# All sixteen gate blocks in seven-product steps, with the attention's filler dealt by eighths

## The chip, the cores and the metric

The kernel runs on one core of a Trainium2 chip. TensorE multiplies matrices (PE in the profile; PEld is its weight load), VectorE (DVE), ScalarE (ACT) and GpSimd (POOL) do the other arithmetic, and SyncE (SP) mostly issues transfers (DMA). Each engine runs its own queue in order and waits for the others by semaphores. The metric is the device time of one execution in microseconds, the median of several runs; lower is better.

## The reference

One layer of a streaming encoder on x of 512 tokens by 1024 features, in float32:

```python
h = rms_norm(x, norm_mix_g)
cb, cc, cin, q, k, v, f_logit, g_logit = split(h @ w_in)      # 3 x 512 | 3 x 512 | 8 | 2 x 1024
y_conv = (cb * causal_dwconv(cc * cin)) @ w_out_conv
o = forgetting_attention(q, k, v, log_sigmoid(f_logit + b_f))   # 8 heads of 64, blocks of 128 queries
y_attn = o @ w_out_attn
g_conv, g_attn = split(sigmoid(g_logit + b_gate))
x = x + (g_conv * y_conv + g_attn * y_attn) @ w_o
h = rms_norm(x, norm_ffn_g)
a, b = split(causal_dwconv(h @ w_up))                          # 2 x 2816
x = x + (silu(a) * b) @ w_down
return rms_norm(x, norm_f_g)
```

## The kernel before

Everything is held transposed, features on the 128 partitions and the 512 tokens along the free axis, so x is eight blocks of 128 x 512. Every product is made of three: weights and activations are split into a high part (a copy rounded to fp32r) and a low part (the difference), and `mm3` (L301) multiplies high by high, low by high and high by low, 256 columns at a time. A weight chunk of 128 x 1024 is loaded by SP into a ring (`load`, L169; four buffers for the tag "raw"), split by ScalarE (L275) and VectorE (L279) in `split`, and used in the order of one list, `stream`.

A *seven-product step* (`seven`, L824) replaces a 2 x 2 arrangement of blocks, which takes eight block products, by seven. Its weights come as P chunks (blocks used as they are) and F chunks (sums of blocks). The sums are made in DRAM ahead of time: `make_forms` (L190) queues for each group of steps a chain of six transfers, alternately a copy issued by SP (`put`, L208) and an adding transfer issued by GpSimd (`add`, L211), and `slot` (L218) releases those that are due by a running count. On the activations' side the step needs the differences of x's quarter blocks, made in `xt` by `x_scale` and `x_sums` during the attention and split into high and low parts `xth` and `xtl` by `x_split` (L899).

The stages in order:

1. *v and forget logits* (L452): x and the weights arrive in eight blocks; TensorE runs some warm-up matmuls on constants first (`NWARM`, L113). The first block's weights come in two transfers, one by ScalarE's queue and one by SP's, and are cast in two pieces.
2. *queries and keys 0 and 1*: four projections of 48 matmuls each.
3. *attention* (L795): 37 slots written out by hand. Slot i issues the scores of unit i (a head and a block of 128 queries), one piece of filler, the transposes of unit i - 3 and, where two query blocks of two heads are complete, the attend of unit i - 5. The filler is a list of halves of projections (24 matmuls): the convolutions' twelve, queries and keys 2 and 3, and the two gate blocks of j = 0 (in20 and in28). GpSimd multiplies the exponentials by the reciprocal of their sum (L625) before the transposes.
4. *gates and mix* (L959): for each of eight j a pair of gate blocks, then `yc` and `ya` (48 matmuls), the sigmoids and the weighted sum. `GJ = 2`: j = 0 takes the gates made in the attention, j = 1 makes them by two plain projections (`p_ga`, `p_gb`), and j = 2 to 7 by a seven-product pair. Temporaries of the gates lie in `xm`, which later holds x again.
5. *w_o*, the second norm (`rstd_col`, `rstd_bc`, L338 to L367: the reciprocal roots are spread over the partitions by matmuls with a broadcast column against the identity), the channel mixer in two phases, the last eight products, and the final norm, among whose steps `warm_on` (L1436) puts matmuls that nobody reads.

TensorE's instructions, the weights' loads and the splits of the first stage are kept in the order of the program (`keep`); the other instructions are placed by the framework. `later`, `run_later` and `flush` hold back evacuation work and release it behind splits.

Of the kernel before, what the change touches and what calls it, by code (L numbers as in the profile page):

```python
# [8 lines left out]
F32 = mybir.dt.float32  # L9
# [4 lines left out]
P = 128  # L14
D = 1024
S = 512
# [11 lines left out]
NWARM = 8  # L28
# [3 lines left out]
PADL, PADR = 16, 120  # L32

# [21 lines left out]
GJ = 2  # L55
# [11 lines left out]
GROUPS = {"gate": (2, 4, 1), "up0": (2, 4, 1), "up1": (2, 4, 1), 0: (2, (0, 3, 14, 18, 22, 26), 1), 1: (2, 3, 1)}  # L67
# [3 lines left out]
def block_kernel(ctx, tc, xT, vecs, wv, win, wmix, wo, wup, wst, wdp, outT):  # L71
# [36 lines left out]

    tbl = cp.tile([4 * H, 1], F32, tag="tbl", name="tbl")
# [14 lines left out]
    late = conv_i[0] + qk_i[2] + conv_i[1] + qk_i[3] + conv_i[2] + conv_i[3] + [20, 28]  # L124
# [8 lines left out]
    for j in range(KB):  # L133
        if j >= GJ:
            stream += step_chunks(n) + step_chunks(n + 1)
            n += 2
        elif j:
# [28 lines left out]
    def tag_of(k):  # L166
        return "raw" if stream[k][0][0] != "F" else "rf" if k >= ff0 else "rg"

    def load(upto):  # L169
        for k in range(len(raws), min(upto, len(stream) - 1) + 1):  # L170
# [10 lines left out]
            else:  # L181
                keep(nc.sync.dma_start(raw[:, :ncol], src if tag == "raw" else made[src]))
# [7 lines left out]
    def make_forms(n0, n1, key, start=0):  # L190

        size, step, shift = GROUPS[key]
        if not start:
            make_forms.slot = 0
# [21 lines left out]
        todo_bg.sort(key=lambda w: w[0])  # L216

# [35 lines left out]
    def split(hl=None):  # L253
# [15 lines left out]
        if k == 0:  # L269
            for cs in (slice(VB, S + H), slice(0, VB)):  # L270
                keep(nc.vector.tensor_copy(hi[:, cs], raw[:, cs]))
# [96 lines left out]

    def rstd_sb(pb, name):
# [17 lines left out]
    xt = yp.tile([P, KB, S], F32, tag="xt", name="xt")  # L387

# [23 lines left out]
    QB = [ap.tile([P, 2, S], F32R, tag=f"qb{i}", name=f"qb{i}") for i in range(2)]  # L412
    KBt = [ap.tile([P, 2, S], F32R, tag=f"kb{i}", name=f"kb{i}") for i in range(2)]
# [6 lines left out]
    def load_x(kb, cs=slice(0, S)):  # L420
        if kb == len(xs):
            if kb % 2 == 0:
                if kb == 4:
                    ap.tile([P, S], F32, tag="pp", name="pp_", bufs=NPP)
                    ap.tile([P, 4], F32, tag="m", name="m_", bufs=6)
                load_x.t = ap.tile([P, 2, S], F32, tag="qt" if kb < 4 else "ka", name=f"xs{kb}", bufs=2)
            xs.append(load_x.t[:, kb % 2, :])
# [12 lines left out]
    keep(nc.gpsimd.dma_start(vec[:, CM:], vecs[:, CM:]))  # L440
# [11 lines left out]
    for kb in range(KB):  # L452
# [18 lines left out]
        for i in squares[kb]:  # L471
            square_x(i)

# [29 lines left out]
    def proj(idx, name, evac, bank):  # L503
        st = {}

        def half(i):
# [7 lines left out]
            if i == 1:  # L514
# [6 lines left out]
        return [lambda: half(0), lambda: half(1)]  # L521
# [4 lines left out]

    AUX = (HD, 0)
# [10 lines left out]
    def evac_qk(pr, isq):  # L538
        def f(p):
# [6 lines left out]
            a = ap.tile([P, 2, S], F32R, tag="qt" if isq else "ka", name=f"a_{nm}", bufs=2)  # L546
# [60 lines left out]
    def scores(pr, e, qb):  # L607
# [15 lines left out]
        )  # L623
        nc.vector.reciprocal(m[:, 2:3], m[:, 1:2])
# [48 lines left out]
    def run_all(fs):  # L673
        for f in fs:
            f()
# [51 lines left out]

    st = []
    f0, f1 = proj(12, "q0", st.append, ring(7))
    f0()  # L730
    rb1 = rstd_sb(rstd_bc(rc1, NT, 6, "n1"), "n1")
# [8 lines left out]
    run_all(proj(16, "k0", st.append, ring(6)))  # L740
# [4 lines left out]
    run_all(proj(13, "q1", evac_qk(1, True), ring(0)))  # L745
    run_all(proj(17, "k1", evac_qk(1, False), ring(1)))
# [35 lines left out]
    fill = []  # L782
    gp = []
    for idx in late:
        kind, i = divmod(idx, 4)
        if idx >= 20:
            ev = gp.append
        else:
            ev = (evac_cb(i), evac_cc(i), evac_cin(i), evac_qk(i, True), evac_qk(i, False))[kind]
        fill += proj(idx, f"in{idx}", ev, acc)  # L790
# [767 lines left out]
```

## Time and profile before

| | |
|---|---|
| median of 3 runs | 691.05 us (690.24 to 692.28) |
| the profiled execution | 690.3 us, of which the span of instructions is 688.5 us |
| granted TensorE clock | 1.000 |
| TensorE busy | 682.0 us, 99% of the span, 5934 matmuls |
| VectorE, ScalarE, GpSimd busy | 555.1, 368.7, 192.3 us |
| attention (53.00 to 182.35) | 129.35 us |
| gates and mix (182.35 to 293.93) | 111.58 us |

Busy time of an engine is the union of its instructions; matmuls overlap in the pipeline, so the spacing of a long run of matmuls (its length divided by their number) says what one costs, not the duration in a row. In a row of groups, `out<-in` names the tiles, `xN` counts the instructions, then come the busy time, the mean duration in ns and, behind a second bar, the idle time before them with what ended it. In a timeline, the two first numbers are start and length in us, and brackets at the end give the idle time before the instruction and what released it.

### The profile page before, as it was taken

What the parts mean: (1) busy time and instruction counts of PE and PEld (TensorE: products, weight loads), DVE (VectorE), ACT (ScalarE), POOL (GpSimd) and SP (SyncE); (2) the same over time, 40 slices, a digit from 0 to 9 for tenths busy, and PEclk for the clock granted to TensorE, in tenths of its full rate; (3) what the DMA queues carried; (4) which work ended last, traced back from release to release, by engine and by line L of the source; (5) the groups of instructions that cost most, each with busy time, mean ns of one, the idle gap of its engine ahead of it and who ended that gap; (6) DMA issues with size and microseconds to landing.
All of it is one profiled execution on the core that took longest, in us unless ns stands there. A gap on an engine that the chain in (4) does not pass through costs nothing.

```text
span 688.5 us, 14711 instructions
## 1 busy us (share of the span) xinstructions
PE 682.0 (99%) x5934; PEld 680.3 (99%) x5934; DVE 555.1 (81%) x860; ACT 368.7 (54%) x582; POOL 192.3 (28%) x204
## 2 busy tenths in 40 slices
PE   9999999999999999999999999999999999999996
PEld 9999999999999999999999999999999999999996
DVE  6677887966578777868869699998887799898895
ACT  5575755555555444446654445545454455455573
POOL 6124947543021201213410144330100313432000
PEclk9999999999999999999999999999999999999999
DMA  9629999562577586788997498889855987776613
GB/s 314 221 62 289 217 241 216 121 141 89 164 171 203 163 264 189 235 317 213 166 316 228 126 240 227 184 248 256 234 170 167 301 257 153 181 187 156 202 41 123
DMA packets 65269, 137.54 MB, mean 200 GB/s; under 512 B 6000, under 2 KB 29952, under 8 KB 64944
## 3 DMA queue, kind: packets, MB, share of 16 engines
q1 hardware_dynamic: 44840, 107.20, 47.1%
q0 software_dynamic: 18912, 26.08, 24.3%
q10 hardware_dynamic: 1448, 3.31, 1.2%
q8 instruction: 46, 0.75, 0.4%
q14 instruction: 23, 0.19, 0.1%
HBM read 132.31 MB, written 47.71 MB: 261 GB/s over the span
## 4 chain that ended last, share of the span: by engine, by line
PE 96%; issue 2%; DVE 1%; POOLq 0%; ACT 0%
PE dn L327 29%; PE p_up L309 21%; PE p_in L309 14%; PE p_up L327 6%; PE p_wo L309 6%; PE yc L309 3%; PE ya L309 3%; PE pa L477 2%; PE pb L479 2%; PE p_q L309 2%; PE p_k L309 2%; PE o L658 2%; PE tp L641 1%; PE s L612 1%; PE p_gb L309 1%
## 5 line engine op out<-in xcount | busy, mean ns | idle before, releaser
L211 POOL DMA_DIRECT2D f<-in_wst_dram x69 | 79.4, 1355 | 26.6 <-DMA f<-f 26.1
L309 PE MATMUL p_up<-x1h,wh_up 128*128 128x256 f32 x416 | 81.1, 276 | 0.0
L309 PE MATMUL p_up<-x1h,wl_up 128*128 128x256 f32 x416 | 81.0, 276 | 0.0
L309 PE MATMUL p_up<-x1l,wh_up 128*128 128x256 f32 x416 | 81.0, 276 | 0.0
L279 DVE TENSOR_TENSOR wl_F<-raw_F,wh_F 128x1024 fp32r<-128x1024 f32 (+1 forms) x43 | 56.1, 1304 | 19.1 <-ACT wh_F L275 19.0
L275 ACT ACTIVATE wh_F<-raw_F 128x1024 fp32r<-128x1024 f32 (+1 forms) x43 | 44.5, 1034 | 40.9 <-PE dn L327 26.5
L309 PEld LDWEIGHTS p_up<-x1h,wh_up 128*128 128x128 f32 x416 | 62.7, 188 | 0.0
L309 PEld LDWEIGHTS p_up<-x1h,wl_up 128*128 128x128 f32 x416 | 62.6, 188 | 0.0
L309 PEld LDWEIGHTS p_up<-x1l,wh_up 128*128 128x128 f32 x416 | 62.6, 188 | 0.0
L309 PE MATMUL p_in<-xgh,wh_in 128*128 128x256 f32 x288 | 56.8, 279 | 0.0
L309 PE MATMUL p_in<-xgh,wl_in 128*128 128x256 f32 x288 | 56.6, 278 | 0.0
L309 PE MATMUL p_in<-xgl,wh_in 128*128 128x256 f32 x288 | 56.5, 278 | 0.0
L1235 POOL TENSOR_TENSOR ge<-fu,fu 128x512 f32<-128x512 f32 x11 | 21.6, 1966 | 124.4 <-DVE fu L570 93.0
L275 ACT ACTIVATE wh_P<-raw_P 128x768 fp32r<-128x768 f32 (+1 forms) x43 | 35.3, 820 | 35.3 <-PE dn L327 23.2
L279 DVE TENSOR_TENSOR wl_P<-raw_P,wh_P 128x768 fp32r<-128x768 f32 (+1 forms) x43 | 41.4, 962 | 15.0 <-ACT wh_P L275 9.1
L327 PE MATMUL dn<-gh,wh_F 128*128 128x256 f32 x216 | 51.1, 276 | 0.0
L327 PE MATMUL dn<-gl,wh_F 128*128 128x256 f32 x216 | 51.0, 276 | 0.0
L279 DVE TENSOR_TENSOR wl_up<-raw_up,wh_up 128x1024 fp32r<-128x1024 f32 x34 | 45.1, 1327 | 6.5 <-ACT wh_up L275 6.4
L275 ACT ACTIVATE wh_up<-raw_up 128x1024 fp32r<-128x1024 f32 x34 | 35.8, 1054 | 22.1 <-PE p_up L309 11.5
L309 PEld LDWEIGHTS p_in<-xgh,wh_in 128*128 128x128 f32 x288 | 44.7, 188 | 0.7
L309 PEld LDWEIGHTS p_in<-xgl,wh_in 128*128 128x128 f32 x288 | 43.7, 188 | 0.0
L309 PEld LDWEIGHTS p_in<-xgh,wl_in 128*128 128x128 f32 x288 | 43.6, 188 | 0.0
(348 smaller groups left out, 2210.8 us busy)
## 6 DMA issues: line engine op xcount, KB each, us to landing
raw_F<-f SPq DMA_DIRECT2D x40, 512.0 KB, 5.8
raw_up<-in_wup_dram SPq DMA_DIRECT2D x34, 512.0 KB, 5.3
raw_P<-in_wst_dram SPq DMA_DIRECT2D x40, 384.0 KB, 5.6
raw_in<-in_win_dram SPq DMA_DIRECT2D x24, 512.0 KB, 3.7
f<-in_wst_dram POOLq DMA_DIRECT2D x41, 256.0 KB, 7.4
f<-in_wst_dram SPq DMA_DIRECT2D x19, 512.0 KB, 7.3
f<-in_wst_dram POOLq DMA_DIRECT2D x19, 512.0 KB, 8.5
f<-f SPq DMA_DIRECT2D x38, 256.0 KB, 6.3
```

The source lines that it names most:

```text
L211: return lambda: keep(nc.gpsimd.dma_start(dst, src, accum_op=ALU.add))
L275: ins = nc.scalar.activation(hi, raw, AF.Copy)
L279: ins = nc.vector.tensor_sub(lo, raw, hi.bitcast(F32))
L309: keep(nc.tensor.matmul(out[:, cs], w, x[:, cs], start=start and i == 0 and c == 0, stop=stop and i == 2 and c == len(cut) - 1,))
L327: keep(nc.tensor.matmul(out, wl if x == 1 else wh, xl if x == 2 else xh, start=opens and bk not in seen, stop=closes and bk not in left,))
L477: keep(nc.tensor.matmul(pa[t][:, :VW], xt, w[:, VB:], start=start, stop=stop))
L479: keep(nc.tensor.matmul(pb[t], xt, w[:, :VB], start=start and t % 2 == 0, stop=stop and t % 2 == 1))
L612: keep(nc.tensor.matmul(s[:, :nn], QT[pr][:, e, qs], KA[pr][:, e, :nn], start=True, stop=False))
L641: keep(nc.tensor.transpose(tp[:, ks], pt[:, ks], ident))
L658: keep(nc.tensor.matmul(o[:, 2 * P * e + c0 : 2 * P * (e + 1)], w, x[:, kb, c0:], start=e == 0 and kb == 0 and i == 0, stop=e == 1 and kb ...
L1235: keep(nc.gpsimd.tensor_mul(ge, a.rearrange(halves_of, h=2), b.rearrange(halves_of, h=2)))
```

## The change

`GJ` becomes 0, so that the gates of all eight j are made by seven-product pairs; the sums for sixteen steps instead of twelve are made in DRAM, in groups whose transfers lie three slots apart instead of four and which start four slots after one another instead of one, from the queries' projections on. in20, in28, in21 and in29 leave the stream. The attention's filler is cut into eighths of a projection (six matmuls) and dealt so that the same share remains in every slot. `x_split` moves from the gate stage into the attention's slots 26, 29, 33 and 34; its results lie in the place of the queries' and keys' tiles (`QB`, `KBt` and the `a` tiles), which in turn lie where the second norm's `x1h` and `x1l` will be, so that x's first copies (`xs`) lie there too. The gates' temporaries move to `xt`, `x1` is a tile of its own and is loaded at j = 4 and 6. The Sigmoid table is loaded in slot 34. In the second norm, ScalarE and VectorE write the reciprocal roots on the diagonal as a high and a low part, and four fp32r matmuls with a matrix of ones spread them. At the start there are two warm-up matmuls fewer, the two halves of the first weights change places, and the rest of the constants `vec` is loaded behind the fifth weight split; at the end the three fillers ahead of the last column sums are gone and five stand behind them instead of six.

```diff
-NWARM = 8
+NWARM = 6
...
+QK = 48
...
-GJ = 2
+GJ = 0
...
-GROUPS = {"gate": (2, 4, 1), "up0": (2, 4, 1), "up1": (2, 4, 1), 0: (2, (0, 3, 14, 18, 22, 26), 1), 1: (2, 3, 1)}
+GROUPS = {"gate": (2, 3, 4), "up0": (2, 4, 1), "up1": (2, 4, 1), 0: (2, (0, 3, 14, 18, 22, 26), 1), 1: (2, 3, 1)}
...
+    onesr = cp.tile([P, P], F32R, tag="onesr", name="onesr")
+    nc.vector.tensor_copy(onesr, ones)
...
-    late = conv_i[0] + qk_i[2] + conv_i[1] + qk_i[3] + conv_i[2] + conv_i[3] + [20, 28]
+    late = conv_i[0] + qk_i[2] + conv_i[1] + qk_i[3] + conv_i[2] + conv_i[3]
...
-            stream += [wi(20 + j), wi(28 + j)]
...
+    k_mix = [c[0] for c in stream].index("mix0")
...
-        return "raw" if stream[k][0][0] != "F" else "rf" if k >= ff0 else "rg"
+        return "raw" if stream[k][0][0] != "F" or k < k_mix else "rf" if k >= ff0 else "rg"
...
-        if not start:
-            make_forms.slot = 0
+        start += make_forms.slot
...
-            for cs in (slice(VB, S + H), slice(0, VB)):
+            for cs in (slice(0, VB), slice(VB, S + H)):
...
+    def rstd_diag(rc, dh, dl):
+
+        for t in range(NT):
+            cs = slice(t * P, (t + 1) * P)
+            nc.scalar.activation(dh[:, cs], ident, AF.Copy, scale=rc[:, t : t + 1])
+            nc.vector.scalar_tensor_tensor(
+                dl[:, cs], ident, rc[:, t : t + 1], dh.bitcast(F32)[:, cs], op0=ALU.mult, op1=ALU.subtract
+            )
+
+    def rstd_rows(dh, dl, bb, name):
+
+        pb = bank(bb, f"pb_{name}")
+        for i, d in enumerate((dh, dl)):
+            for cs in (slice(0, 2 * P), slice(2 * P, S)):
+                keep(nc.tensor.matmul(
+                    pb[:, cs], onesr, d[:, cs],
+                    start=i == 0 and cs.start == 0, stop=i == 1 and cs.start > 0,
+                ))
+        return pb
...
+    xp0 = ctx.enter_context(tc.tile_pool(name="xp0", bufs=1, side="right"))
+
+    def x_tiles(a, b):
+        h = xp0.tile([P, KB, S], F32R, tag="x1h", name=a)
+        l = xp0.tile([P, KB * S + PADR], F32R, tag="x1l", name=b)
+        return h, l, l[:, : KB * S].rearrange("p (a b) -> p a b", b=S)
+
+    xp0.tile([P, KB, S], F32R, tag="x1h", name="x1h_")
+    xs_all = xp0.tile([P, KB * S + PADR], F32, tag="x1l", name="xs")
+    QPOS = (0, 2, 1, 3)
+    KOFF = 4 * S + QK
...
-    QB = [ap.tile([P, 2, S], F32R, tag=f"qb{i}", name=f"qb{i}") for i in range(2)]
-    KBt = [ap.tile([P, 2, S], F32R, tag=f"kb{i}", name=f"kb{i}") for i in range(2)]
...
-    keep(nc.gpsimd.dma_start(vec[:, CM:], vecs[:, CM:]))
...
+        if kb == 4:
+            with after_split():
+                keep(nc.gpsimd.dma_start(vec[:, CM:], vecs[:, CM:]))
...
-                    for part in (0, 1):
+                    for part in (1, 0):
...
-            for kb in range(4 * i, 4 * i + 4):
+            for kb in range(KB * i // n, KB * (i + 1) // n):
...
+    xth, xtl_, xtl = x_tiles("xth", "xtl")
+    QB = [xth[:, 2 * i : 2 * i + 2, :] for i in range(2)]
+    KBt = [xth[:, 2 * i : 2 * i + 2, :] for i in (2, 3)]
...
-            a = ap.tile([P, 2, S], F32R, tag="qt" if isq else "ka", name=f"a_{nm}", bufs=2)
+            a = pair_of(xtl_, (pr % 2) * 2 * S + (0 if isq else KOFF))
...
+    make_forms(0, len(GATES), "gate")
...
-    run_all(proj(16, "k0", st.append, ring(6)))
+    run_slots(proj(16, "k0", st.append, ring(6)))
...
-        take = 1 if i < n + LA - 1 else len(fill)
-        for _ in range(min(take, len(fill))):
...
+    def x_split(q):
+        def f():
+            p = QPOS[q]
+            nc.scalar.activation(xqh[:, p], xq[:, q], AF.Copy)
+            nc.vector.tensor_sub(xql[:, p], xq[:, q], xqh.bitcast(F32)[:, p])
+
+        return f
...
+    GSETS = (1, 3, 0, 4)
...
+        fill += proj(idx, f"in{idx}", ev, acc, KB)
...
+    XS = (26, 29, 33, 34)
...
+        if i in XS:
+            flush_only([("q", x) for x in range(4)])
+            with after_split():
+                x_split(XS.index(i))()
...
+        if i == n + 2:
+            nc.scalar.activation(tbl, scores.sum[: 4 * H], AF.Sigmoid)
+        while len(fill) * (n + LA - 1) > nf * max(n + LA - 2 - i, 0):
+            fill.pop(0)()
...
+    acc = ring(2, 5, 6, 7)
...
-    xm = xp.tile([P, KB, S], F32, tag="x1", name="xm")
+    x1 = xp.tile([P, KB, S], F32, tag="x1", name="x1")
...
-        if j == KB - 1:
-            assert mt.n == 3 * KB
-            x1 = xm
-            nc.gpsimd.dma_start(x1[:, :4, :], xT[:, :4, :])
-        if j == 0:
-            evac_gate(0, gs)(gp[0])
-            evac_gate(8, gs)(gp[1])
-        elif j < GJ:
-            run_all(proj(20 + j, f"ga{j}", evac_gate(j, gs), acc))
-            run_all(proj(28 + j, f"gb{j}", evac_gate(8 + j, gs), acc))
-        else:
-            if j == GJ:
-                acc = ring(3, 4, 2, 7)
-            seven(GATES[2 * (j - GJ) : 2 * (j - GJ) + 2], 2 * (j - GJ), {j: (0, 1, 5, 6)}, gate_form, done=gate_pair(j, gs))
+        if j in (4, 6):
+            nc.gpsimd.dma_start(x1[:, 2 * j - 8 : 2 * j - 4, :], xT[:, 2 * j - 8 : 2 * j - 4, :])
+        gs = []
+        seven(GATES[2 * j : 2 * j + 2], 2 * j, {j: GSETS}, gate_form, done=gate_pair(j, gs))
...
-    nc.gpsimd.dma_start(x1[:, 4:, :], xT[:, 4:, :])
...
-                    nrm["c"] = rstd_col([ssq2], NT, 6, "n2")
+                    nrm["d"] = [t[:, 0:2, :].rearrange("p a b -> p (a b)") for t in (gh, gl)]
+                    rstd_diag(rstd_col([ssq2], NT, 6, "n2"), *nrm["d"])
 
                 def late():
-                    nrm["b"] = rstd_sb(rstd_bc(nrm["c"], NT, 7, "n2"), "n2")
+                    nrm["b"] = rstd_sb(rstd_rows(*nrm["d"], 7, "n2"), "n2")
...
     sqB = fin_sum(1, 1)
-    warm_on(3)
     rcB = fin_col(1, [sqB])
-    warm_on(6)
+    warm_on(5)
```

More of the change, by code (lines that the diff above doesn't have):

```diff
@@ L216, in make_forms @@
         todo_bg.sort(key=lambda w: w[0])
+    make_forms.slot = 0
     def slot():
@@ L500, in block_kernel, with proj, part @@
                     rc1 = rstd_col([ssq], NT, 6, "n1")
-    def proj(idx, name, evac, bank):
+    def proj(idx, name, evac, bank, n=2):
         st = {}
-        def half(i):
+        def part(i):
             if i == 0:
@@ L519, in half @@
                     evac(st["p"])
-        return [lambda: half(0), lambda: half(1)]
+        return [lambda i=i: part(i) for i in range(n)]
+    xth, xtl_, xtl = x_tiles("xth", "xtl")
+    QB = [xth[:, 2 * i : 2 * i + 2, :] for i in range(2)]
+    KBt = [xth[:, 2 * i : 2 * i + 2, :] for i in (2, 3)]
     AUX = (HD, 0)
@@ L623, in scores @@
         )
+        scores.sum = m[:, 1:2]
         nc.vector.reciprocal(m[:, 2:3], m[:, 1:2])
@@ L780, in block_kernel @@
         k += 4
[L782 to L787, printed above, removed]
-        else:
-            ev = (evac_cb(i), evac_cc(i), evac_cin(i), evac_qk(i, True), evac_qk(i, False))[kind]
-        fill += proj(idx, f"in{idx}", ev, acc)
-    units = [(pr, e, qb) for pr in range(4) for hf in range(2) for qb in (2 * hf, 2 * hf + 1) for e in range(2)]
-    LT, LA = 3, 5
-    n = len(units)
-    make_forms(0, len(GATES), "gate")
-    for i in range(n + LA):
-        slot()
-        if i < n:
-            scores(*units[i])
-        take = 1 if i < n + LA - 1 else len(fill)
-        for _ in range(min(take, len(fill))):
-            fill.pop(0)()
-        if 0 <= i - LT < n:
-            transp(*units[i - LT])
-        if 0 <= i - LA < n:
-            pr, e, qb = units[i - LA]
-            if e == 1 and qb % 2 == 1:
-                attend(pr, qb // 2)
-    assert not todo_bg
-    at.close()
+    xqh, xql = (t.rearrange("p (q b) (h c) -> p q (b h) c", b=2, h=2) for t in (xth, xtl))
     halves_of = "p (h c) -> p h c"
@@ L956, in gate_pair @@
         return done
+    GSETS = (1, 3, 0, 4)
+    fill = []
+    for idx in late:
+        kind, i = divmod(idx, 4)
+        ev = (evac_cb(i), evac_cc(i), evac_cin(i), evac_qk(i, True), evac_qk(i, False))[kind]
+        fill += proj(idx, f"in{idx}", ev, acc, KB)
+    nf = len(fill)
+    units = [(pr, e, qb) for pr in range(4) for hf in range(2) for qb in (2 * hf, 2 * hf + 1) for e in range(2)]
+    LT, LA = 3, 5
+    XS = (26, 29, 33, 34)
+    n = len(units)
+    for i in range(n + LA):
+        slot()
+        if i in XS:
+            flush_only([("q", x) for x in range(4)])
+            with after_split():
+                x_split(XS.index(i))()
+        if i < n:
+            scores(*units[i])
+        if i == n + 2:
+            nc.scalar.activation(tbl, scores.sum[: 4 * H], AF.Sigmoid)
+        while len(fill) * (n + LA - 1) > nf * max(n + LA - 2 - i, 0):
+            fill.pop(0)()
+        if 0 <= i - LT < n:
+            transp(*units[i - LT])
+        if 0 <= i - LA < n:
+            pr, e, qb = units[i - LA]
+            if e == 1 and qb % 2 == 1:
+                attend(pr, qb // 2)
@@ new lines, in block_kernel @@
+    assert not fill and not todo_bg
+    at.close()
+    acc = ring(2, 5, 6, 7)
+    xp = ctx.enter_context(tc.tile_pool(name="xp", bufs=1, side="right"))
+    x1 = xp.tile([P, KB, S], F32, tag="x1", name="x1")
+    hg = ExitStack()
+    hp = hg.enter_context(tc.tile_pool(name="hp", bufs=1, side="right"))
+    mh = hp.tile([P, KB, S], F32R, tag="mh", name="mh")
+    ml = hp.tile([P, KB, S], F32R, tag="ml", name="ml")
+    for i in range(2):
+        hp.tile([P, S], F32, tag="sq", name=f"sq2_{i}_", bufs=2)
```

68 lines of the change are left out of this document (19 added, 49 removed).

## The prediction

> **What bounds the kernel now.** I read the busy table of the page first, then the waits of TensorE, then the chain that ended last in order of time, and last the stages the change touches.
>
> ```profile
> span 688.5 us, 14711 instructions
> PE 682.0 (99%) x5934; PEld 680.3 (99%) x5934; DVE 555.1 (81%) x860; ACT 368.7 (54%) x582; POOL 192.3 (28%) x204
> PE warm L115 <- DVE ones L107: 1.1, 1, 1.1
> ...
> 53.00 2.76 PE p_in L309 x24
> ...
> 180.54 1.81 PE o L658 x16
> ...
> 187.85 5.44 PE p_ga L309 x48
> 193.29 5.44 PE p_gb L309 x48
> ...
> 204.17 9.52 PE dn L327 x84
> ...
> 349.44 0.89 PE pb_n L363 x8
> ```
>
> Busy time of TensorE can hide pipelining; what decides is that its whole list of waits is one line of 1.1 us, before the first warm-up, and that the chain from 53.00 to 349.44 is TensorE piece after piece. So a matmul that is left out shortens the kernel by its spacing, as long as the other engines keep up with the faster pace. A matmul of 256 columns is spaced 9.52 / 84 = 113.3 ns in the gate stage and 2.76 / 24 = 115.0 ns between the attention's pieces.
>
> **The gates.** Gates 0 are two plain projections dealt into the attention (96 matmuls of its 864, the p_in group has three forms of 288); gates 1 are the 96 of p_ga and p_gb. Both become a seven-product pair of 84 like that at 204.17.
>
> - attention: 129.35 us from 53.00 to 182.35, less 96 x 0.115 = 11.04: 118.3 us;
> - gate stage: + 9.52 for j = 0, and 9.52 instead of 10.88 for j = 1: + 8.16;
> - together **-2.88 us**.
>
> This holds if the rest of the attention fits into 118.3 us. Busy times by stretch (start:end, length, then TensorE, weight load, VectorE, ScalarE, GpSimd, granted clock, DMA share):
>
> ```profile
> 53.00:182.35 129.35, 129.35 (x1103) 128.66 (x1103) 98.05 (x218) 74.31 (x164) 65.24 (x78) 1.00 0.75 180
> ...
> 70.00:100.00 30.00, 30.00 (x258) 29.82 (x257) 25.48 (x56) 19.30 (x44) 21.80 (x27) 1.00 1.01 220
> ...
> L902 DVE TENSOR_TENSOR xtl<-xt,xth 128x1024 fp32r<-128x1024 f32 x4 | 4.8, 1211 | 0.0
> L279 DVE TENSOR_TENSOR wl_in<-raw_in,wh_in 128x1024 fp32r<-128x1024 f32 x18 | 22.6, 1256 | 4.7 <-ACT wh_in L275 4.7
> ```
>
> VectorE is nearest: 98.05 us. It loses three weight splits there (in20, in28, mix0), gains those of P0 and F0, all priced as wl_in (1.26), and the four x_split differences (4 x 1.21): 98.05 - 1.26 + 4.84 = 101.6 of 118.3 us, 86%. Before, 25.48 of 30 us, 85%, went by without a stall. Dealing by eighths gives 128 / 36 = 3.6 eighths (21.3 matmuls) to a slot instead of 24; a slot falls from about 3.6 to 3.3 us, and the projections' own vector work spreads over 36 slots instead of 32. ScalarE (74.31, with four copies and a table load to come, rows below) is near 67%. I charge nothing for the middle.
>
> The distance from a normalised row to its transposes is the other cover:
>
> ```profile
> 124.01 0.48 POOL L625 TENSOR_SCALAR pp<-pp,m 128x256 f32<-128x256 f32 x1 [1.61 <-DVE m L624]
> ...
> 130.35 0.38 PE L641 MATMUL tp<-ident,pp 128*128 128x128 f32 x2
> ...
> f<-in_wst_dram POOLq DMA_DIRECT2D x6, 512.0 KB, 11.1
> f<-f SPq DMA_DIRECT2D x12, 256.0 KB, 6.5
> f<-in_wst_dram POOLq DMA_DIRECT2D x12, 256.0 KB, 7.0
> SPq L208 <- DMA f<-in_wst_dram: 22.9, 10, 3.5
> L211 POOL DMA_DIRECT2D f<-in_wst_dram x18 | 27.4, 1590 | 0.3 <-issue 0.2
> ```
>
> That unit's row was ready at 124.49 and used at 130.35, 5.9 us later, the shortest but for the first units; three slots of 3.3 us leave about 4.9. GpSimd issues 24 adding transfers for the gate weights' sums instead of 18, 6 x 1.59 = 9.5 us more, so about 75 us of 118, the first of them already in the stage of queries and keys. The steps of one group now lie 3 slots = 9.9 us apart, before 4 x 3.6 = 14.6. An add lands in 7.0 to 11.1 us and a put in 6.5, so SP's puts, which waited 22.9 us in ten waits already, will wait more, and the weight loads queued behind them with them; those loads are four buffers (some 28 us) ahead. Fewer groups run side by side (18 adds over 36 slots' first two thirds before, 24 over all now), so landings should not grow. Cost 0; without the 4.9 us of cover each late row would cost TensorE what exceeds it.
>
> **The attention's tail.** The last slots now carry the x_split of the last two quarters, the table load and the splits of P0 and F0.
>
> ```profile
> 177.19 0.60 PE L641 MATMUL tp<-ident,pp 128*128 128x128 f32 x4
> 177.83 0.60 ACT L644 ACTIVATE pth<-tp 128x512 fp32r<-128x512 f32 x1 [1.44 <-PE tp L641]
> 178.46 0.69 DVE L645 TENSOR_TENSOR ptl<-tp,pth 128x512 fp32r<-128x512 f32 x1 [0.57 <-ACT pth L644]
> 185.84 1.28 ACT L892 ACT_TABLE_LOAD   x1 [1.25 <-DVE xm L891]
> ...
> 189.33 1.04 ACT L901 ACTIVATE xth<-xt 128x1024 fp32r<-128x1024 f32 x1
> ```
>
> The last attend (180.54) had its input at 179.15, 1.4 us of slack. One x_split copy (1.04), the table load (1.28) and its dummy (0.2) stand ahead of the last pth: 2.5 us, of which 1.44 fill ScalarE's idle time; the slot loses 0.3. So the stall is between 0 and 1.4 us. I take **+0.3**: nearer the zero, since in before's row ScalarE waits for TensorE there and not the reverse. What becomes late next is nothing: yc0 and ya0, which read this end, come 9.52 us later than before. The table load is gone from j = 0, where nothing waited on it.
>
> **The second norm.** rstd_bc's eight half-passes (0.89 us) become four fp32r matmuls of 256 columns, 4 x 0.113 = 0.45: **-0.44**. New are four ScalarE and four VectorE instructions on 128x128.
>
> ```profile
> 343.44 1.04 POOL L356 TENSOR_TENSOR rc_n<-ms_n,ex 128x4 f32<-128x4 f32 x1 [1.39 <-DVE ms_n L354]
> 344.44 1.23 DVE L1079 TENSOR_TENSOR gl<-y,gh 128x1024 fp32r<-128x1024 f32 x1 [1.08 <-ACT gh L1076]
> 29.58 0.37 ACT L714 ACTIVATE v<-pb,rc_n 128x128 fp32r<-128x128 f32 x1 [2.69 <-PE pb L479]
> 30.22 0.34 DVE L715 SCALAR_TENSOR_TENSOR v<-pb,rc_n,v 128x128 fp32r<-128x128 f32 x1
> ```
>
> From rc at 344.48, ScalarE needs 4 x 0.37 = 1.5; VectorE, free at 345.67, 4 x 0.34 = 1.4: ready near 347.2, needed at 349.44 - 0.44 or so. Hidden by 1.8 us of p_up; behind them queue wh_P and wl_P (346.76, 347.64), which move by less than that.
>
> **The start and the end.**
>
> ```profile
> L115 PE MATMUL warm<-ones x16: 421/421/580, 1.1 to 4.4; 128*128 128x128 f32 x16
> L363 PE MATMUL pb_n<-ident,rc_n x24: 270/275/276, 32.2 to 682.5; 128*128 128x128 f32 x24
> ...
> L479 PE MATMUL pb<-wh_v,xgh x4: 278/280/343, 5.4 to 6.1; 128*128 128x256 f32 x4
> 4.04 1.20 DVE L271 CAST wh_v<-raw_v 128x264 fp32r<-128x264 f32 x2 [3.04 <-DMA raw_v<-in_wv_dram]
> 7.79 0.43 DVE L273 CAST wh_v<-raw_v 128x520 fp32r<-128x520 f32 x1 [1.02 <-DMA raw_v<-in_wv_dram]
> 8.36 0.36 PE L477 MATMUL pa<-wh_v,xgh 128*128 128x264 f32 x1
> 681.82 0.17 DVE L352 RECIPROCAL rc_n<-ms_n 128x2 f32<-128x2 f32 x1 [1.26 <-ACT ms_n L350]
> 682.14 0.61 PE L363 MATMUL pb_n<-ident,rc_n 128*128 128x128 f32 x4
> ...
> POOL xm L989 <- DVE xm L988: 104.8, 8, 17.9
> ```
>
> Both halves of the first weights are cast in one go (4.04, two casts in 1.20 us), so their order there and in the matmuls is worth about nothing. The second block starts at 8.36 on weights that land at 7.79; taking the constants' transfer out of the way (it goes behind the fifth weight split, with its first readers in the forget gates, two stages on) can bring that forward by at most the 0.33 us that the first block leaves (its 24 matmuls at 0.12 end some 2.9 us after 5.1). Against it: all sixteen warm-up records ran at 421 ns where the same form takes 275 later, so the array is slow until after 4.4 us; sixteen starts in 3.3 us are 0.22 apart, so four records fewer end near 3.9, with a gap of 0.7 before the first cast lets TensorE begin at about 4.7. If the array is then still slow, the first block's 24 matmuls cost more: between -0.33 and +1.8 (next part). I take 0, the two being opposed. The Trainium skill, TensorE: Matmul & The Clock Gate, Part 1, says that the array runs at half clock until a free-running window of about 3.4 us has been busy; this trace agrees with a slow stretch of 3.4 us or more. By that rule twelve warm-up records can be too few, and the sum would be up to 1.8 us higher: rival 2.
>
> At the end the reciprocal frees pb_n at 681.99, and pb_n starts at 682.14: the fillers lie inside waits for ScalarE and VectorE. Cost 0 either way. The x1 loads move to earlier gate steps on GpSimd's queue, which waits 104.8 us for VectorE there; first readers come after the stage: 0. Halves of x in the queries' and keys' place are the same instructions at other addresses, 0; the F0 and F1 loads use the ordinary ring, and F2, the first that must wait for attention's memory, is needed some 15 us after it: 0.
>
> **Sum**: -2.88 - 0.44 + 0.3 = **-3.0 us**. The profiled execution took 690.3 (span 688.5 and 1.8 around it), so 687.3; the median of the runs, 691.05, stands 0.75 above it: **688.0**.
>
> **Rivals.** A change of 0.3%, 2.1 us, is about what this measurement can tell from none, so 689.0 is the border of faster.
>
> 1. *The tail is given back.* If ScalarE's queue blocks behind the last convolution (a ScalarE tap waits for GpSimd 1.7 us on average in before, four waits of 6.9 us in sum), the 1.4 us stall is joined by that 1.7: 688.0 - 0.3 + 3.1 = 690.8 at worst, 689.5 for half. For it: four jobs move into slots of 2.8 us. Against: VectorE and ScalarE are only half busy in that stretch before. Same.
>
> ```profile
> 173.00:182.35 9.35, 9.35 (x84) 9.35 (x83) 4.73 (x8) 3.88 (x6) 0.00 (x0) 1.00 0.39 113
> ACT u L566 <- POOL z L587: 6.9, 4, 2.5
> ```
>
> 2. *The array starts slow.* The slow stretch lasted from 1.05 to between 4.4 and 5.4 us (the pb rows). If it begins anew at about 4.7, up to 4.3 us of matmuls run at half pace, 2.1 us lost, less the 0.33 us in which the second block waits anyway: + 1.8, 689.8. For it: the gap of 0.7 us. Against: most of a stretch is fed before. Same.
> 3. *GpSimd held by the sums: slower.* If the adds' landing grows so that a group's step falls behind its 9.9 us by more than the 4.9 us of cover, GpSimd stands in front of the normalising instructions and TensorE waits, once for each of 8 groups; half of it I count as made up by later cover. It decides from a landing of 9.9 + 4.9 + 1.3 = 16.1 us on (8 x 1.3 / 2 = 5.2, past 693.1); at 17 us it is 8 x 2.2 / 2 = 8.8: 696.8. For it: a DMA share of 1.01. Against: landings of 7 to 11 us.
>
> **Chances.** Forecast (687.0 to 689.0) 0.66; rival 1 0.15; rival 2 0.11; rival 3 0.06; a better start than bounded 0.02. Faster 0.67, same 0.26, slower 0.07. The likeliest case alone runs from 686.7 (start -0.33, no stall, and half the spread of runs) to 689.2 (stall 1.4); the range takes in most of rivals 1 and 2: 686.6 to 690.2.
>
> **What would show it.** Right: p_in x768 and dn on xgh/xth x672 instead of 864 + 96 and 504; the attention 118 to 119 us long with TensorE's waits still empty; pb_n of four fp32r matmuls near 0.45 us; the second block of v at or before 8.36. Wrong: waits of TensorE on ptl or on pp; pth of the last unit starting more than a microsecond after its transposes; v's first block with matmuls above 400 ns; GpSimd's L211 waiting on f. The prediction fails if the attention is longer than 120 us or the first 9 us grow by more than one.

## The result: 12 us slower, with the attention 15.7 us longer than forecast

The changed kernel takes 702.8 us (median of four runs, 702.65 to 703.38) against 690.6 for the kernel before on the same chip: a ratio of 1.0174, interval 1.0162 to 1.0187. The forecast was 688.0, with 690.2 as its upper end. The profiled execution took 702.8 us, its span 701.0 (before: 690.3 and 688.5). Of all the executions below one lies far from the others of its kernel and is left out, 1393.05 us in the run whose sums are dealt as before and begun early.

The busy table of the page after:

```profile
span 701.0 us, 14706 instructions
...
PE 681.6 (97%) x5898; PEld 678.1 (97%) x5898; DVE 566.2 (81%) x879; ACT 374.0 (53%) x593; POOL 198.1 (28%) x210
```

TensorE is as busy as before (682.0) in a span 12.5 us longer. Its waits (line waited for: us in total, times, longest):

```profile
PE s L648 <- ACT pp L657: 9.0, 3, 8.0
PE s L648 <- POOL xtl L591: 2.4, 1, 2.4
PE warm L118 <- DVE ones L108: 1.1, 1, 1.1
PE pb L512 <- DVE wh_v L274: 0.8, 1, 0.8
PE s L649 <- DVE xth L592: 0.2, 1, 0.2
```

The one line of before has become five. Three of them, 9.0 + 2.4 + 0.2 = 11.6 us, stand in front of the attention's scores. SP's longest sum of waits, and then GpSimd's for copies, within the attention:

```profile
SPq L209 <- DMA f<-in_wst_dram: 78.4, 12, 16.8
```

```profile
POOL f L212 <- DMA f<-f: 11.7, 2, 7.3
```

SP's copies waited 22.9 us for adds before and wait 78.4 now; GpSimd's adds, which waited for no transfer there before, wait 11.7 us for copies between the sums. From the chain that ended last, in order of time (start, length, what), the first gate pair and the second norm:

```profile
187.18 9.59 PE dn L330 x84
...
362.43 0.46 PE pb_n L386 x4
```

By stage, from the first score in the timeline to the ends of the stages in the chain (the first product of the gate stage, the first of w_o, the end of the span):

| us | before | forecast | after |
|---|---|---|---|
| up to the first score | 52.60 | 52.60 | 52.52 |
| attention | 129.75 | 119.0 | 134.66 |
| gates and mix | 111.58 | 119.74 | 119.75 |
| the rest of the span | 394.57 | 394.13 | 394.07 |

The gate stage grew as forecast (9.59 us for the first 84 products, priced at 9.52), and the second norm cost 0.46 for the 0.45 forecast. The attention is 4.9 us longer than before and 15.7 us longer than forecast. 11.6 of these are the waits; some 2.3 more were lost in a stretch of lower clock behind the longest wait, and the rest, under 2 us, is not placed here. Three stretches of 10 us (columns as in the prediction; the granted clock is the third number from the end):

```profile
73.00:83.00 10.00, 10.00 (x89) 10.00 (x87) 3.99 (x10) 4.28 (x9) 6.54 (x8) 1.00 0.84 208
83.00:93.00 10.00, 1.96 (x11) 1.72 (x10) 1.57 (x3) 2.74 (x6) 5.12 (x7) 0.68 0.79 163
93.00:103.00 10.00, 9.43 (x65) 9.19 (x65) 9.61 (x22) 7.73 (x19) 5.53 (x8) 0.81 0.95 156
```

The rows of SP, GpSimd, VectorE, ScalarE and TensorE in the timeline around the longest wait (in brackets the idle time before the instruction and what ended it):

```profile
81.60 0.47 SPq L209 DMA_DIRECT2D f<-f  x1
...
87.88 1.05 POOL L212 DMA_DIRECT2D f<-in_wst_dram  x1 [7.34 <-DMA f<-f]
88.53 1.70 POOL L633 TENSOR_TENSOR y<-y,u 128x512 f32<-128x512 f32 x1
...
77.42 0.13 DVE L653 DVE_READ_ACCUMULATOR2_ANT m<- 128x1 f32 x1
...
90.26 0.63 ACT L634 ACTIVATE ych<-y 128x512 fp32r<-128x512 f32 x1 [12.94 <-POOL y L633]
90.80 0.35 ACT L657 ACTIVATE pp<-s,m 128x128 f32<-128x128 f32 x1
...
91.29 0.58 PE L648 MATMUL s<-xtl 128*128 128x256 f32 x1 [8.04 <-ACT pp L657]
```

Read from below: TensorE waits 8.04 us for a bank of scores, which is free only when an exponential (`pp<-s`) has read it. That exponential's input was there at 77.55 (the row of m), but it ran at 90.80, because ScalarE stood at `ych` for 12.94 us. `ych` waited for the product y, which stood on GpSimd behind an add; the add waited 7.34 us for a copy, and the copy went out on SP at 81.60, when the add before it had landed. This copy is not slow: from 81.60 to 87.88 are 6.3 us with the issue. Four queues, each in order, hand one delay on.

The Trainium skill, "TensorE: Matmul & The Clock Gate", in its opening table, calls ScalarE, VectorE and GpSimd strict first-in-first-out queues. The trace agrees: the exponential was ready for 13.25 us behind an instruction that was not.

### The profile page after: what moved, and what is told of

It is laid out like the page before. It is cut to its first block, busy times and chain, and to the rows that moved or that the text cites. A ratio compares the mean times of both kernels' runs of the same rounds, so it can differ in the third digit from the quotient of the medians.

```text
span 701.0 us, 14706 instructions
## 1 busy us (share of the span) xinstructions
PE 681.6 (97%) x5898; PEld 678.1 (97%) x5898; DVE 566.2 (81%) x879; ACT 374.0 (53%) x593; POOL 198.1 (28%) x210
## 4 chain that ended last, share of the span: by engine, by line
PE 82%; DMA 6%; DVE 5%; issue 3%; ACT 2%; POOL 0%; SPq 0%; POOLq 0%; ACTq 0%; DVEq 0%
PE dn L330 31%; PE p_up L312 20%; PE p_in L312 7%; PE p_up L330 6%; PE p_wo L312 6%; DMA f<-in_wst_dram 3%; PE ya L312 3%; PE yc L312 3%; DMA f<-f 2%; PE pa L510 2%; PE pb L512 1%; DVE wl_in L282 1%; PE o L695 1%; ACT wh_in L278 1%; DMA xs<-in_xT_dram 1%
## 5 line engine op out<-in xcount | busy, mean ns | idle before, releaser
L282 DVE TENSOR_TENSOR wl_F<-raw_F,wh_F 128x1024 fp32r<-128x1024 f32 (+1 forms) x47 | 61.9, 1316 | 19.9 <-ACT wh_F L278 19.8
L278 ACT ACTIVATE wh_F<-raw_F 128x1024 fp32r<-128x1024 f32 (+1 forms) x47 | 48.7, 1037 | 39.1 <-PE dn L330 26.2
L278 ACT ACTIVATE wh_P<-raw_P 128x768 fp32r<-128x768 f32 (+1 forms) x47 | 38.7, 822 | 34.7 <-PE dn L330 24.0
L282 DVE TENSOR_TENSOR wl_P<-raw_P,wh_P 128x768 fp32r<-128x768 f32 (+1 forms) x47 | 45.5, 968 | 14.1 <-ACT wh_P L278 6.9
L312 PE MATMUL p_in<-xgh,wh_in 128*128 128x256 f32 x256 | 51.6, 283 | 0.0
L312 PE MATMUL p_in<-xgh,wl_in 128*128 128x256 f32 x256 | 51.4, 282 | 0.0
L312 PE MATMUL p_in<-xgl,wh_in 128*128 128x256 f32 x256 | 51.1, 281 | 0.0
L312 PEld LDWEIGHTS p_in<-xgh,wh_in 128*128 128x128 f32 x256 | 40.9, 193 | 0.7
L330 PEld LDWEIGHTS dn<-gl,wh_F 128*128 128x128 f32 x216 | 40.5, 188 | 0.0
L330 PEld LDWEIGHTS dn<-gh,wh_F 128*128 128x128 f32 x216 | 40.5, 188 | 0.0
```

The costliest lines, as they stand in the source:

```text
L278: ins = nc.scalar.activation(hi, raw, AF.Copy)
L282: ins = nc.vector.tensor_sub(lo, raw, hi.bitcast(F32))
L312: keep(nc.tensor.matmul(out[:, cs], w, x[:, cs], start=start and i == 0 and c == 0, stop=stop and i == 2 and c == len(cut) - 1,))
L330: keep(nc.tensor.matmul(out, wl if x == 1 else wh, xl if x == 2 else xh, start=opens and bk not in seen, stop=closes and bk not in left,))
```

## The experiments

Theory A: the transfers that make the gates' sums hold GpSimd (and SP), and the others wait for these in order. Theory B: VectorE and ScalarE are too full in an attention that gives them less time. Theory C: the new start costs time. Ratios are to the kernel before on the same chip, with the 95% interval. Differences in us between two runs are of medians, and the medians of the kernel before lay between 690.30 and 691.02 us in the sessions; so such a difference can be off by some 0.7 us.

**The dealing of the sums.** Only `GROUPS["gate"]` (group size, slots between steps, slots between groups) and the place of `make_forms` are changed:

```diff
 # e1: (2, 4, 1), make_forms moved to the attention; e7: (2, 4, 1), early
 # g1: (2, 5, 2), early; e2: the kernel before with (2, 3, 4)
-"gate": (2, 3, 4)
+"gate": (2, 4, 1)
```

> The changed kernel, except that the eight groups of sums are dealt as the kernel before deals its six: a group's steps four slots apart, groups one slot after another, begun with the attention's first slot and not with the queries' projections. Theory A (the chain of sums: a copy on SP's queue waits for the add before it, the next add on GpSimd's queue waits for that copy, and ScalarE and TensorE stand behind GpSimd): the wait of 8.0 us and the 2.6 us that 24 matmuls lost at the half clock behind it go, 702.8 - 8.0 - 0.6 - 2.6 = 691.6, with the wait of 2.4 us on key 3 left. Theory B (VectorE and ScalarE are too full in the shorter attention, and the sums only show it): within a microsecond of 702.8, the stall at another place.

> The kernel before with one number changed: its six groups of sums are dealt with steps three slots apart and groups four slots after one another, still begun with the attention. Theory A: GpSimd stands at an add while its copy is under way and TensorE waits; between 2 us (the first group alone) and 11 us are lost, 693 to 702. Theory B: the attention of before is 129 us long and has room, so 690.6.

> The changed kernel with the sums' steps four slots apart and groups one slot after another, begun early as the changed kernel does. Theory A with the order of the dealing as its cause: 691.6, as with the late start. Theory A with the early start as its cause (eight copies and adds among the queries' and keys' weights and rows): the stall comes earlier, between 45 and 70 us, and 695 to 703. Theory B: within a microsecond of 702.8.

> The changed kernel with all eight groups, begun early, but a group's steps five slots apart (some 16.5 us for 9.9) and the groups two slots after one another. If the step is too short for a copy and the add that waits for it (SP's copies wait 8 to 9 us for an add, then land in 6 to 9 us), GpSimd no longer stands at an add: 691 to 694. If the attention is too full, or the eight groups too many, whatever the step: 698 or more.

| run | us | ratio |
|---|---|---|
| before's dealing, begun with the attention | 707.9 | 1.0247 (1.0232 to 1.0262) |
| before's dealing, begun early | 716.33 | 1.0379 (1.0361 to 1.0397) |
| steps of five slots, begun early | 700.3 | 1.0132 (1.0116 to 1.0147) |
| kernel before with the new dealing | 690.45 | 0.9999 (0.9989 to 1.0009) |

The form of theory A that blames the dealing fell: none of the three repairs it, and the new dealing does no harm to the kernel before. (Of the run begun early with before's dealing no profile is read here.) Two of them show where the time goes instead. Two adds in the chain of the run begun with the attention:

```profile
72.32 13.54 DMA f<-in_wst_dram
...
86.14 16.54 DMA f<-in_wst_dram
```

With eight groups one slot behind another the adds run side by side and land after 13.5 and 16.5 us. With steps of five slots the rows of GpSimd, ScalarE and TensorE around TensorE's longest wait are these:

```profile
83.94 2.17 POOL L212 DMA_DIRECT2D f<-in_wst_dram  x2 [6.94 <-DMA f<-f]
85.50 1.90 POOL L633 TENSOR_TENSOR y<-y,u 128x512 f32<-128x512 f32 x1
...
87.44 0.63 ACT L634 ACTIVATE ych<-y 128x512 fp32r<-128x512 f32 x1 [8.50 <-POOL y L633]
87.97 0.35 ACT L657 ACTIVATE pp<-s,m 128x128 f32<-128x128 f32 x1
...
88.47 0.58 PE L648 MATMUL s<-xtl 128*128 128x256 f32 x1 [3.60 <-ACT pp L657]
```

It is the chain of the changed kernel again: an add waits 6.94 us for a copy, `ych` 8.50 us for the product behind that add, and TensorE 3.60 us for the exponential behind `ych`. A weight load issued at 76.44 lands at about the same time, 11.16 us later, but the split that reads it stands behind that exponential in ScalarE's queue.

**Fewer sums.**

```diff
+            if key == "gate" and g >= NSUM:
+                for n in range(a, b):
+                    made[n] = wst[n, :, 3 * m : 7 * m]
+                continue
 # e8: NSUM = 0; e10: 6; f4: 6, late start; g2: 6, late start, (2, 4, 1)
```

> The changed kernel without the sums for the gates: the F chunks are loaded from the weights as they lie, at the same size, so that the 48 transfers of the eight groups fall away (left out of the computation: these sums). Theory A (the sums' transfers hold GpSimd and SP): the first stall goes whole, 702.8 - 8.0 - 0.6 - 2.6 = 691.6, with the wait of 2.4 us on key 3 left; GpSimd never waits for f. Theory B (VectorE and ScalarE too full): TensorE still waits for pp or ptl, 697 or more.

> The changed kernel with the sums of the first six groups alone, dealt at the same times; the last two groups' F chunks are loaded as they lie (left out of the computation: their sums). Theory A by volume (eight groups in an attention of 118 us are more than the transfers carry, six are not): like the run without sums, 691 to 693. Theory A by the start (the first groups run into SP's and GpSimd's queues at 45 to 90 us, whatever comes later): the stall at 83 us stays, 699 to 703.

> The changed kernel with the sums of six groups alone at the changed kernel's spacing, as in the run with six groups, but begun with the attention and not with the queries' projections (left out of the computation: the sums of two groups). In the kernel before this dealing of six groups cost nothing. If the early start did the harm (a copy of the second group stood on SP's queue behind the rows of f until 48 us, and the group's chain ran late from there): 691 to 693. If the shorter attention did it, with as many sums in 118 us as before in 129: 697 or more.

> The changed kernel with the sums of six groups alone, dealt exactly as in the kernel before (four slots, one slot, begun with the attention; left out of the computation: the sums of two groups). Step too short: 691 to 694, as it is four slots again. Fuller attention (each slot 3.3 us for 3.65): 697 to 701, as with six groups at three and four slots.

In these four runs the sums of all or of two groups are left out of the computation. The attention without any sums as one stretch:

```profile
54.21:177.90 123.69, 121.75 (x1012) 120.04 (x1011) 99.69 (x219) 77.07 (x168) 41.88 (x60) 0.99 0.26 81
```

Without the sums the kernel takes 692.4 us (1.0029, 1.0017 to 1.0040): of 12.1 us, some 10 go with these 48 transfers, and VectorE's load is the same (99.69 us here, 100.19 in the changed kernel, below) in an attention 11 us shorter. This speaks for A and against B as the main cause. With six groups the time is 699.4 (1.0127, 1.0112 to 1.0142), begun with the attention 700.0 (1.0132, 1.0117 to 1.0148), and dealt exactly as in the kernel before 702.75 (1.0174, 1.0157 to 1.0191). So it is not the number of sums alone: what costs nothing in the kernel before costs 12 us here.

**GpSimd cleared.** The adds stay, the products and the normalising behind them go; the copies of queries and keys stay.

```diff
-            nc.gpsimd.tensor_mul(y, y, cst[i])
+            nc.vector.tensor_mul(y, y, cst[i])       # and z: e3, e9
-        nc.gpsimd.tensor_scalar(pt, pt, m[:, 2:3], ...)
+            nc.scalar.activation(pt, pt, AF.Copy, scale=m[:, 2:3])   # e9, one slot later
```

> The changed kernel with the convolution's two products (y by u, and z by cc, eight instructions of 128 x 512) on VectorE and not on GpSimd, so that ScalarE does not wait for GpSimd there; the sums are dealt as in the changed kernel. Theory A: the 8.0 us are paid through ScalarE's wait for y (12.9 us), which is gone; what is left is that GpSimd stands up to 7.3 us before the normalised rows, of which 4.9 us are covered: 702.8 - 11.2 + 2.4 = 694, between 692 and 698. Theory B: VectorE gets eight times about 1.2 us more and the kernel gets slower, 703 to 710.

> The changed kernel with all its sums, but with GpSimd's arithmetic taken away from behind the adds: the convolution's products go to VectorE and the normalising of the exponentials to ScalarE (one slot later, as Copy with a scale per row); on GpSimd stay the adds and the copies of queries and keys. Theory A in its form that GpSimd's own queue is the place where the time is lost: 691 to 694. If SP's queue (weights behind copies that wait for adds) or the memory's bandwidth is the place: TensorE waits for wl_in instead and 696 to 703. Theory B: ScalarE gets 32 times about 0.5 us more, 703 or more.

With the products alone moved the kernel takes 698.0 us (1.0112, 1.0087 to 1.0137); with the normalising moved too, 692.9 (1.0032, 1.0020 to 1.0044), as without sums. GpSimd's waits for copies in the cleared kernel's attention, then the two longest of TensorE, the second of them in the first stage:

```profile
POOL f L212 <- DMA f<-f: 63.5, 9, 13.1
```

```profile
PE s L648 <- POOL xtl L591: 1.8, 1, 1.8
PE pa L510 <- DVE wh_v L276: 1.3, 1, 1.3
```

GpSimd now waits 63.5 us for copies, five times as long as in the changed kernel, and the kernel is 10 us faster: a wait on GpSimd costs by what stands behind it. The same transfers run here as in the changed kernel, so neither they nor a shared bandwidth cost the time by themselves.

**Key 3.** TensorE's remaining wait in front of the scores (`s<-xtl`) is for copies of key 3. Its projection comes earlier in the filler, first without sums, then with the clearing, then with the old start too, then with `x_split`'s differences on GpSimd:

```diff
-    late = ... + conv_i[1] + qk_i[3] + conv_i[2] + conv_i[3]
+    late = ... + conv_i[1][:2] + qk_i[3] + conv_i[1][2:] + conv_i[2] + conv_i[3]
```

> The same, and in the filler's order queries and keys 3 change places with the last of convolution 1's three projections, so that key 3's projection ends some 2.3 slots (7 us) earlier. If the wait of 2.4 us on key 3's copies comes from the filler's dealing by eighths, it goes: 2 to 2.4 us below the run without the reordering, 689.2 by theory A. If it comes from GpSimd being late by the sums, the two runs are the same.

> Both repairs on the changed kernel with all its sums: GpSimd's arithmetic cleared from behind the adds (products to VectorE, normalising to ScalarE) and key 3's projection 2.3 slots earlier. Theory A (the sums hold GpSimd; key 3's wait from the eighths): the wait of 1.8 us on key 3 and the 1.7 us of half clock behind it go from the cleared kernel's 692.9, and 689.4 to 690.7 is left, as without sums. Theory B (ScalarE and VectorE now too full): 692 or more.

> The same with the start of the kernel before: eight warm-up matmuls, the first weights' halves, the first block's order and the constants' transfer as they were. Theory C (with six warm-ups the array stands idle before its first block, and in part of the runs that block then goes at half pace): 0.5 to 1.2 us below the run without this, 688.5 to 690.0. If the start is worth nothing either way: within 0.4 us of that run.

> The version with both repairs and the old start, with x_split's four subtractions (128 x 1024) on GpSimd, which is idle from 150 us on there. In that version TensorE waits 2.2 us at 156 us for an exponential behind a row of VectorE's instructions with one such subtraction of 1.1 us in it. If this is VectorE's load in those slots: 691.9 - 2.2 = 689.0 to 690.0. If the wait only moves to the next thing in VectorE's row: within 0.5 us of 691.9.

Without sums the reordering takes 1.7 us off (690.7; 1.0001, 0.9989 to 1.0013): the wait on key 3's copies is the dealing by eighths, whose last piece for key 3 falls in slot 22, before its first use in slot 24. With the sums and the clearing it gains nothing (693.1; 1.0040, 1.0027 to 1.0052): the wait on key 3 goes, and TensorE waits 2.27 us at 157 us for an exponential behind VectorE. With the old start 691.9 (1.0018, 1.0010 to 1.0027). With the differences on GpSimd 693.1 (1.0032, 1.0020 to 1.0045): that wait falls to 1.1, and waits of 1.1 and 0.5 appear before the last attends. What is left, 1.2 to 2.8 us by the ratios, fits theory B, but the clearing itself put the products on VectorE and the normalising on ScalarE, so it does not show B for the changed kernel. No version tried beats the kernel before.

**The start.**

```diff
 # f3, on the kernel before: NWARM 8 -> 6, order of the halves and of the first block, vec's load
```

> The kernel before with the new start alone (six warm-ups, halves and order of the first block exchanged, constants behind the fifth split). Theory C: median 0.4 to 1.5 us above the kernel before, single runs 1.7 above. My prediction's bound for the start was -0.33 to +1.8 with 0 taken: within 0.4 us.

691.2 (1.0009, 1.0000 to 1.0018): 0.2 us above the kernel before by the medians, not told from nothing. On the cleared kernel the old start brought 1.2 us (693.1 to 691.9), as theory C has it, so the start is worth between 0 and 1.2 us against the change, most of which the medians cannot show. The profiles show more. Two rows of the first block in the kernel without sums:

```profile
8.50 0.63 PE L517 MATMUL pb<-wh_v,xgl 128*128 128x256 f32 x2
8.93 0.64 PE L515 MATMUL pa<-wh_v,xgl 128*128 128x264 f32 x2
```

The pairs are still 0.43 us apart there, where they are 0.24 apart in the changed kernel, and the first score comes at 54.21 instead of 52.52. The same is seen in five of the fourteen profiles with the new start that are read here (without sums, cleared with key 3 early, six groups begun with the attention, steps of five slots, filler in halves) and in none of the five with the old start. This is the prediction's rival 2; it did not come in the changed kernel's profile.

**The filler.**

```diff
 # g3: halves for eighths
-        fill += proj(idx, f"in{idx}", ev, acc, KB)
+        fill += proj(idx, f"in{idx}", ev, acc)
 # h2: two projections more, read by nobody
-    late = conv_i[0] + ... + conv_i[3]
+    late = conv_i[0] + ... + conv_i[3] + [20, 28]
 # h1, on the kernel before (and the places of its temporaries)
-GJ = 2
+GJ = 1
```

> The changed kernel with its sums as they are, but the filler dealt in halves of projections (24 matmuls) in place of eighths, by the same rule, so that four or five of the slots get none. If the dealing by eighths puts the evacuations where GpSimd stands: below 698. If the sums do it: 700 to 706, with the bare slots as new waits.

> The kernel before with GJ = 1: the gates of j = 1 by a seven-product pair too (seven groups of sums in place of six, dealt as before), those of j = 0 still as filler in an attention of 129 us. By the spacing of before, 96 x 0.1133 - 9.52 = 1.36 us go. If the attention's length is what hides the sums: 690.6 - 1.4 = 689.2, and up to 690.6 where x_split is late for j = 1's F chunk. If the seventh group is what is too much: stalls in the attention, 693 or more.

> The changed kernel with two projections more in its filler (the gate weights 20 and 28, whose products nobody reads), so that each slot has 24 matmuls of filler again and the attention's work on TensorE is that of the kernel before, 129.35 us; the sums as in the changed kernel. If the shorter attention is what uncovers the sums: the attention takes 129.4 to 132 us, and the whole 697 to 700. If the eight groups or the new places of x, queries and keys do it: stalls as before, the attention takes 140 us or more, the whole 706 to 714.

With the filler in halves the kernel takes 699.9 us (1.0137, 1.0123 to 1.0150), and the stalls are still there. With the filler given back it takes 699.2 us (1.0122, 1.0108 to 1.0137), with all eight groups, the changed dealing and the new places of x, queries and keys. All its waits of TensorE:

```profile
PE warm L118 <- DVE ones L108: 1.1, 1, 1.1
PE pb L512 <- ACT xgh L488: 0.9, 1, 0.9
PE pb L512 <- DVE wh_v L274: 0.8, 1, 0.8
```

GpSimd's wait for the sums' transfers in its attention, and the chain at the attention's two ends:

```profile
POOL f L212 <- DMA f<-in_wst_dram: 3.0, 1, 3.0
```

```profile
54.10 0.12 PE s L648
...
183.73 9.59 PE dn L330 x84
```

The attention as one stretch, with the filler given back and then in the changed kernel:

```profile
54.10:183.73 129.63, 129.63 (x1105) 128.93 (x1105) 102.56 (x223) 79.32 (x170) 71.00 (x83) 1.00 0.86 203
```

```profile
52.52:187.18 134.66, 123.01 (x1011) 120.90 (x1010) 100.19 (x219) 76.80 (x167) 68.57 (x82) 0.96 0.84 190
```

The attention has no wait left and lasts 129.63 us, at full clock (129.80 from the first score in the timeline, at 53.93, as in the table). Take its 96 unread products away at 0.115 us and 118.8 remain, beside the forecast's 119.0. With 11 us of work more on TensorE the attention is 5 us shorter (129.63 for 134.66), although SP's copies still wait 60.6 us for adds. The 2.7 matmuls more of filler in each slot (864 / 36 = 24, for 768 / 36 = 21.3) hide the sums. The edit does more than lengthen the slots: it loads and splits two weights more, and it deals the other pieces four to a slot, so that key 3's last falls in slot 19 instead of 22. Of that order key 3 alone was tested, worth 1.7 us.

The step of one more seven-product pair in the kernel before (the attention at 129 us) did not gain its 1.4 us: 695.2 (1.0073, 1.0053 to 1.0094). There is one wait in the attention, and `x_split` comes late for j = 1, where two waits follow:

```profile
PE dn L327 <- DVE xtl L902: 1.9, 1, 1.9
PE tp L641 <- DVE ptl L645: 1.6, 1, 1.6
...
PE dn L327 <- ACT xth L901: 0.8, 1, 0.8
```

The wait of 1.6 us stands behind a full row of VectorE's instructions, and GpSimd waits only 1.1 us for a copy in this attention. So this run does not show that a seventh group is too much: the larger part of its waits, 2.7 us, is for `x_split` behind the attention.

## Why the prediction was wrong

**The step that failed** is "I charge nothing for the middle", with the "Cost 0" behind it. It was mis-sized by 15.7 us. Without any sums the attention takes 123.6 us (54.21 to 177.80), and with key 3 earlier too 121.4 (52.52 to 173.95), for the 119.0 forecast and 134.7 measured. So some 11 us go with the sums' transfers, 2 with the place of key 3, and 2.4 remain that no run took away without giving TensorE more work. Four parts of the step were wrong or not looked up:

1. *The cover.* I took the way from a normalised row to its transposes, 4.9 us, for all that depends on GpSimd. The same queue makes y and z, for which ScalarE waits (z: 6.9 us in four waits, a row that I had quoted for the tail). A late y stops not its own consumer alone but each exponential and weight split behind it on ScalarE. Moving the two products alone took 4.8 us off the kernel, moving the normalising too 9.9.
2. *Busy shares.* VectorE came to 100.19 us, where I had worked out 101.6, and 86% "went by without a stall" before. The share was right and proved nothing. The cleared kernel, the one without sums and the one with the filler given back all carry about as much on VectorE, and stall little or not at all.
3. *The weights.* "Four buffers (some 28 us) ahead" was not looked up in a row. TensorE waits for no weight within the attention in any profile read here, so no run shows that this part cost time.
4. *The dealing by eighths.* I counted it as a relief for VectorE and priced nothing against it. It brings key 3's last piece to slot 22, two slots before its first use, and TensorE waits for it (2.4 us in the changed kernel, 1.5 without sums).

A slip without effect: four slots of 3.6 us are 14.4 us, not 14.6.

**Rival 3** named the right queue, with a chance of 0.06, and the wrong point. It needed landings of 16.1 us; it came with landings that had not grown (median of the 512 KB adds in the attention 10.0 us, 11.1 before); 16.5 us was seen in the run with before's dealing. I priced the landing of one transfer, and what grew was the number of queues that pass a wait on: a put waits in SP's queue for an add, the next add in GpSimd's for the put, `ych` in ScalarE's for GpSimd.

**What held.** The gate stage (+8.17 us for +8.16), the second norm (-0.43 or so for -0.44), the attention's tail (no wait before the last attends, for the +0.3 taken), p_in at 768 matmuls, the second block of v at 8.33, under 8.36, and "the prediction fails if the attention is longer than 120 us". With the 96 products subtracted, the run with the filler given back would stand at 699.2 - 11.0 = 688.2, an estimate, as no such kernel ran, beside the forecast's 688.0. Its profile has 1.4 us of late start in it (first score at 53.93 for 52.52), so the sum of the other terms was right to some 1.5 us.

**What stays open.** Shown is that the sums' transfers carry the loss, that it is paid through what stands behind the adds on GpSimd, and that 24 matmuls of filler in a slot hide it and 21.3 do not. That a slot of 3.3 us turns the queues' order into a loop that never catches up is argued from the chain; which link tips first was not the same in all runs (GpSimd's adds wait for copies between the sums in the changed kernel, and not with six groups begun with the attention), and no run varied the slot's length between the two.

## What to carry to other kernels

A matmul taken out of a stage that TensorE bounds is a gain only as long as the stage's other chains fit into what is left: for every in-order queue, follow what is behind each instruction that can wait, and whose queue waits for that. Work that hides transfers is worth keeping, or the transfers' waits must first be put on a queue with nothing behind them. When clearing a queue of other work makes its waits longer and the kernel faster, that queue was the place.

## What the hardware showed that I had not expected

A short wait of TensorE can cost as much again in clock. Rows of TensorE with the wait in brackets, followed by the next pairs of equal matmuls, in the kernel without sums, then in the cleared ones with key 3 early (new start, old start):

```profile
134.88 0.38 PE L653 MATMUL s<-xtl 128*128 128x256 f32 x1 [1.47 <-POOL xtl L596]
...
136.48 0.63 PE L317 MATMUL p_in<-xgh,wh_in 128*128 128x256 f32 x2
136.91 0.63 PE L317 MATMUL p_in<-xgh,wl_in 128*128 128x256 f32 x2
```

```profile
159.16 0.74 PE L648 MATMUL s<-xtl 128*128 128x512 f32 x1 [2.27 <-ACT pp L657]
...
160.12 0.63 PE L312 MATMUL p_in<-xgh,wh_in 128*128 128x256 f32 x2
160.55 0.63 PE L312 MATMUL p_in<-xgh,wl_in 128*128 128x256 f32 x2
```

```profile
158.98 0.50 PE L646 MATMUL s<-xtl 128*128 128x512 f32 x1 [2.24 <-ACT pp L655]
...
159.55 0.39 PE L312 MATMUL p_in<-xgh,wh_in 128*128 128x256 f32 x2
159.78 0.39 PE L312 MATMUL p_in<-xgh,wl_in 128*128 128x256 f32 x2
```

Behind a wait of 1.47 us pairs of matmuls are 0.43 us apart for 3.4 us (136.1 to 139.5), where 0.23 is usual, so some 1.6 us are lost; so too behind 2.27 us, but not behind 2.24 us. The wait's length alone does not decide it. In the changed kernel the stretch behind the wait of 8.04 us lasted from 91.29 to 96.9, some 2.3 us lost.

The Trainium skill, "TensorE: Matmul & The Clock Gate", Part 1, says that the clock falls back after at least one idle window of about 3.4 us. These rows differ: a wait of 1.47 us was enough once, and 2.24 us was not another time. They fit what the same part says of the window, that it runs free of the kernel; that its phase decided between 2.27 and 2.24 us is not shown.
